# Gate and output projections computed token-major in 512-column groups, in a two-layer decoder kernel on one core

## The chip, the cores and the metric

The kernel runs on one core of one Trainium2 chip. The metric is the device time of one execution in microseconds, as the median of several runs. The engines are called as the profile calls them: PE is TensorE (matmuls; PEld its weight loads), DVE is VectorE, ACT is ScalarE, POOL is GpSimd, SP is SyncE, which issues most DMAs.

## What is computed

Two decoder layers over 256 tokens of width 2048: a gated-linear-attention layer with its ConvFFN, then a cross-attention layer with its ConvFFN. The parts that matter here are the output gate `g` and the two projections back to the residual:

```python
xn = rms_norm(x, norm_w)
proj = xn @ w_in
q, k, v, g = jnp.split(proj, [...], axis=-1)          # g: 2048 columns
...
o = rms_norm(o, o_norm_w) * jax.nn.silu(g.astype(f32)).reshape(B, S, H, dv)
return o.reshape(B, S, GLA_VAL_DIM).astype(x.dtype) @ w_out     # gla_w_out, 2048 x 2048
...
o = o.transpose(1, 0, 3, 2, 4).reshape(B, S, H * Dh)
return o @ w_out                                               # moba_w_out, 2048 x 2048
...
h = h + mixer(...)
h = h + conv_ffn(h, ...)
```

## The kernel before

**Precision.** Every large product is made from split operands: an activation `x` is kept as a high and a low part, side by side, and so is every weight tile. Three of the four products are formed: high weight with both parts of `x`, low weight with the high part.

**Weights.** `WeightStream` loads all weights in one fixed sequence of 1 MB DMAs issued by SP (three raw buffers). A *step* consumes half of such a load, 1024 columns per partition. Before a step's matmuls ACT copies the raw half into `whi` (L144) and DVE subtracts to make `wlo` (L146). Both have four buffers, so the halves for step n can be made when PE has finished with those of step n - 4. `step()` also runs the jobs that are due: `after(k, job)` puts a job k steps ahead. A planner orders the instructions of each engine when the program is built; each engine then runs its list strictly in order.

**Two ways of a product.** `gemm` (L366, L368) is feature-major: the weight is the stationary operand and the result has features on partitions, two blocks of 128 features (a *pair*) by 256 tokens. Its high-weight matmul has 512 moving columns (both parts of 256 tokens), its low-weight one 256. A pair takes four steps. `gemm_tok` (L381, L384) is token-major: the activation is stationary, the weight moves with 512 columns, and the result has tokens on partitions, two tiles of 128 tokens by 512 features. A group of 512 columns takes eight steps. Results lie in `acc` (three buffers in PSUM). Token-major are the v, q, k and kv projections and the two up-projections; feature-major are k and q of the first layer, its gate, and both output projections.

**Turning.** The up-projection turns its token-major result: ACT scales each tile by the tokens' rstd (L720), DVE transposes it in 32 x 32 squares (L722), and `square` (L705) puts the squares in their place with 16 copies on POOL. The rest of the work on it runs 8 and 11 steps later (`UP_LAG`).

**The gate**: for each of eight pairs ACT copies and DVE adds the two halves of `acc` (`both`), DVE multiplies by rstd, ACT applies Silu, DVE multiplies by the head's rstd and by `o` with its norm weight (L627, L629), and `split` makes the operand `go` of the next product (L406, L407).

**The projections** (`project`): for each of eight pairs `residual` adds both halves of `acc` to `h` (L402, L403) and `feed` makes the next norm's operand (`make_xw`, L258, L262) and adds the squares. `Norm.close` makes the rstd from the sum of squares with two matmuls of one column (L307). The operands of a norm are a list in the order of feeding.

**Beside it** `make_ahead` loads parts of `w_dn` every nine steps (`ahead`, two buffers), forms differences on DVE (L329, L330) in four of the steps 5 to 8 after, and writes them back from POOL's queue (`tsum`, L339). `park` writes `h` out on POOL's queue.

Of the kernel before, what the change touches and what calls it, by code (L numbers as in the profile page):

```python
# [18 lines left out]
S = 256  # L19
KT = D // 128  # L20
NP = KT // 2
KD = 1024
VD = 2048
GH = 4
# [7 lines left out]
C_GN, C_KVN, C_MN, C_FN, C_ON, C_KN, C_QN, C_CW = 0, 16, 32, 48, 80, 84, 85, 86  # L32
# [10 lines left out]

UP_LAG = (8, 11)
EARLY = (1, 3)
ASIDE = (5, 7, 9, 11, 13, 15, 16)
# [107 lines left out]


@with_exitstack
def trunk(ctx: ExitStack, tc: tile.TileContext, xT, cst, msk, w1p, w2a, w_k, w_qa, w_v2, w_v, w_g, w_go,
          w_up0, w_dn0, w_kk, w_kv, w_mq, w_mo, w_up1, w_dn1, rel, onehot, out):  # L160
    nc = tc.nc
    V, A, T = nc.vector, nc.scalar, nc.tensor

# [27 lines left out]
    plan = [(w_v2, 1, 16384), (w_v, 2, 8192), (w_k, 4, 4096), (w_qa, 4, 4096), (w_g, 8, 4096), (w_go, 8, 4096),  # L191
            (w_up0, FT // 2, 8192), (w_dn0, 2, None),
            (w_mq, 4, 8192), (w_kk, 4, 8192), (w_kv, 4, 8192), (w_mo, 8, 4096),
            (w_up1, FT // 2, 8192), (w_dn1, 2, None)]
    for w, groups, cols in plan:
        for g in range(groups):
# [8 lines left out]
    h = [hs[p // 2][:, p % 2] for p in range(NP)]  # L205
# [44 lines left out]
    def col(c):  # L250
        return gn[:, c - C_GN:c - C_GN + 1] if C_GN <= c < C_GN + KT else cs[:, c:c + 1]

    def make_xw(p, c, name):
        x = slot([128, 2, 2 * S], F32R, name)
        for i in range(2):
            n = col(c + 2 * p + i)
            if ws.x_low:
                hi = A.activation(x[:, i, :S], h[p][:, i, :], AF.Copy, scale=n)  # L258
                ws.first = ws.first or hi.ins
            else:  # L260
                V.tensor_scalar(x[:, i, :S], h[p][:, i, :], n, None, op0=OP.mult)  # L261
# [59 lines left out]
    def after(steps, job):  # L321
        later.append((cur[0] + steps, job))
# [36 lines left out]
    def gemm(xs, kts):  # L359

        ps = acc_ps.tile([128, 2, 512], F32, name="acc")
        for q0 in range(0, kts, 8):
            two = [step(), step(1)]
            tiles_ = [(q0 + 4 * i + k, b, i, k * 256 + b * 128) for i in range(2) for k in range(4) for b in range(2)]
            for kt, b, i, c in tiles_:
                T.matmul(ps[:, b, :], two[i][0][:, c:c + 128], xs(kt), start=kt == 0, stop=False)  # L366
            for kt, b, i, c in tiles_:
                T.matmul(ps[:, b, :S], two[i][1][:, c:c + 128], xs(kt)[:, :S], start=False, stop=kt == kts - 1)  # L368
        ws.prefetch(cur[0])
        return ps  # L370

    def gemm_tok(xs, groups=1):
        out_ = [acc_ps.tile([128, 2, 512], F32, name="acc") for _ in range(groups)]
        for q0 in range(0, KT, 2):
            for ps in out_:
                hi, lo = step()
                for ks in ((0,), (1,)) if cur[0] < 5 and groups > 1 else ((0, 1),):
                    tiles_ = [(q0 + k, t, k * 512) for k in ks for t in range(2)]
                    for x0 in (0, S):
                        for kt, t, c in tiles_:  # L380
                            T.matmul(ps[:, t, :], xs(kt)[:, x0 + 128 * t:x0 + 128 * t + 128], hi[:, c:c + 512],  # L381
                                     start=kt == 0 and x0 == 0, stop=False)
                    for kt, t, c in tiles_:
                        T.matmul(ps[:, t, :], xs(kt)[:, 128 * t:128 * t + 128], lo[:, c:c + 512],  # L384
                                 start=False, stop=kt == KT - 1)
        ws.prefetch(cur[0])
        return out_ if groups > 1 else out_[0]

    def rows(xs):
        return lambda kt: xs[kt // 2][:, kt % 2, :]  # L390

    def both(ps, name):
        t = temp(name)
        A.copy(t, ps[:, :, S:])
        V.tensor_add(t, t, ps[:, :, :S])
        return t

    def bc(r):
        return r[:, None, :S].to_broadcast([128, 2, S])
# [5 lines left out]
    def split(dst_hi, dst_lo, src):  # L405
        A.copy(dst_hi, src)  # L406
        V.tensor_sub(dst_lo, src, dst_hi.bitcast(F32))  # L407

    class Norm:


        def __init__(self, c, name, rows=True, columns=False):
            self.c, self.name, self.rows, self.columns, self.xs = c, name, rows, columns, []
            self.acc = keep.tile([128, 2, S], F32, name="acc_sq", tag="acc_sq")

        def operand(self, p):
            self.xs.append(make_xw(p, self.c, self.name))

        def feed(self, p):
            self.operand(p)  # L420
# [10 lines left out]
    nrm = Norm(C_GN, "xw", columns=True)  # L431
# [12 lines left out]
    xs = rows(nrm.xs)  # L444
# [81 lines left out]
    for hd in (2, 3):  # L526
        ps = gemm_tok(xs)
# [39 lines left out]
    heads = [{} for _ in range(GH)]  # L567
# [39 lines left out]
    for hd in range(GH):  # L607
        ps = gemm(xs, KT)
# [8 lines left out]
        for lag, job in ((2, gla_scores), (4, gla_values), (6, gla_norm)):  # L617
            after(lag, lambda job=job, hd=hd: job(hd))

    go = []  # L620
    for hd in range(GH):
        for c in range(2):
            ps = gemm(xs, KT)
            g = both(ps, "g")
            V.tensor_mul(g, g, bc(rstd))
            A.activation(g, g, AF.Silu)
            V.tensor_mul(g, g, bc(heads[hd]["r"]))  # L627
            for i in range(2):
                V.scalar_tensor_tensor(g[:, i, :], heads[hd]["o"][:, 2 * c + i, :], col(C_ON + 2 * c + i),  # L629
                                       g[:, i, :], op0=OP.mult, op1=OP.mult)  # L630
            gx = slot([128, 2, 2 * S], F32R, "go")
            split(gx[:, :, :S], gx[:, :, S:], g)
            go.append(gx)

    def project(xs, kts, norms):
# [58 lines left out]
    def combine_parts(k, hid, kept):  # L694
# [5 lines left out]
    def square(y, x):  # L700

        for m in range(4):
            xs_ = x[32 * m:32 * m + 32].rearrange("a t (n c b) -> a n t c b", c=4, b=32)
            for c in range(4):
                nc.gpsimd.tensor_copy(y[32 * c:32 * c + 32, :, :, 32 * m:32 * m + 32], xs_[:, :, :, c])  # L705

    def ffn(layer, nrm, then):
        xs = rows(nrm.xs)
# [5 lines left out]
        def turn_up(g, ps):  # L714
# [10 lines left out]
            for jj in range(2):  # L725
                after(UP_LAG[jj], lambda jj=jj: conv(g, jj, y[:, jj]))

# [350 lines left out]
    xs = rows(n_q.xs)  # L1078
    for g in range(4):
        ps = gemm_tok(xs)  # L1080
# [8 lines left out]
    xs = rows(xkv)  # L1089
    for g in range(4):  # L1090
        ps = gemm_tok(xs)
# [11 lines left out]
    for g in range(4):  # L1103
        ps = gemm_tok(xs)
# [121 lines left out]
```

## Time and profile before

| | us |
|---|---|
| Median of 3 runs | 2176.6 (2175.9 to 2176.62) |
| Profiled execution | 2175.2 |
| Its span, first to last instruction | 2173.4 |
| First output projection, first matmul to the next stage's first | 296.93 to 385.99 |

The granted TensorE clock is 1.00 throughout. The page lists busy times by engine; the chain that ended last follows the work back from the end and says which engine set the time at each moment. A group of instructions is shown as line, engine, operation, output and input, count, then busy time and mean length in ns, then the idle time before it with what ended that idle time. An instruction's length is longer than the distance to the next one where they overlap; the distance between starts is called the pitch here.

### The profile page before, as it was taken

To read this page: it belongs to the slowest core of one execution; us is meant where nothing else is said; L and a number is where in the kernel's file an instruction comes from. 1 tells how busy PE (TensorE), PEld (TensorE's weight loads), DVE (VectorE), ACT (ScalarE), POOL (GpSimd) and SP (SyncE) were. 2 spreads that over 40 slices of the span, in tenths; PEclk is the share of its full clock that TensorE was granted. 3 is DMA by queue.
4 is the path that set the end of the run, shared out by engine and by line. 5 is a ranking of instruction groups with operands and counts; after the bars stand their busy time and mean duration, and the time that the engine had idled before them with its cause. 6 is when DMAs were issued, how large, how long until landed. Compare 5 with 4: busy or idle time off the path is not lost.

```text
span 2173.4 us, 29230 instructions
## 1 busy us (share of the span) xinstructions
PE 2165.5 (100%) x10224; PEld 1815.1 (84%) x10224; DVE 1829.8 (84%) x2531; ACT 1311.9 (60%) x1849; POOL 659.4 (30%) x925
## 2 busy tenths in 40 slices
PE   9999999999999999999999999999999999999999
PEld 7889888888888888887888888888888888888887
DVE  7676877699999897977978787677999999979898
ACT  6655655456565655766756666445565656567575
POOL 0000000264656464300001343003655565542000
PEclk9999999999999999999999999999999999999999
DMA  7575778777778785887967788677787878759896
GB/s 289 209 289 178 263 263 321 287 263 285 273 281 313 275 311 191 329 329 259 366 245 293 275 299 294 228 285 276 284 302 275 310 284 290 293 191 349 325 358 251
DMA packets 113526, 613.01 MB, mean 282 GB/s; under 512 B 29361, under 2 KB 29889, under 8 KB 49634
## 3 DMA queue, kind: packets, MB, share of 16 engines
q1 hardware_dynamic: 94610, 523.75, 66.5%
q0 software_dynamic: 18048, 86.60, 10.5%
q8 instruction: 80, 1.31, 0.2%
q10 hardware_dynamic: 720, 0.79, 0.1%
q14 instruction: 68, 0.56, 0.1%
HBM read 535.31 MB, written 75.78 MB: 281 GB/s over the span
## 4 chain that ended last, share of the span: by engine, by line
PE 98%; DMA 2%; DVE 0%; ACT 0%; issue 0%; ACTq 0%; DVEq 0%; SPq 0%
PE acc L381 40%; PE acc L384 20%; PE acc L803 13%; PE acc L366 11%; PE acc L368 6%; PE p L803 5%; DMA wraw<-w_dn 1%; PE sT L577 0%; DMA sums<-tsum 0%; DMA ahead<-tsum 0%; PE tr L1005 0%; PE s L1023 0%; DVE wlo L146 0%; DMA h<-xT 0%; PE z L483 0%; PE o L463 0%
## 5 line engine op out<-in xcount | busy, mean ns | idle before, releaser
L146 DVE TENSOR_TENSOR wlo<-wraw,whi 128x1024 fp32r<-128x1024 f32 (+1 forms) x788 | 954.3, 1221 | 266.6 <-ACT whi L144 179.8
L144 ACT CAST whi<-wraw 128x1024 fp32r<-128x1024 f32 (+1 forms) x788 | 797.1, 1018 | 611.9 <-PE acc L381 361.8
L381 PE MATMUL acc<-whi,xw 128*128 128x512 f32 x3328 | 825.5, 389 | 0.6 <-DVE xw L261 0.6
L381 PEld LDWEIGHTS acc<-whi,xw 128*128 128x128 f32 x3328 | 623.5, 188 | 130.4 <-issue 1.1
L705 POOL COPY up<-uT 32x256 f32<-32x256 f32 x704 | 520.9, 740 | 310.5 <-DVE uT L722 240.7
L384 PE MATMUL acc<-wlo,xw 128*128 128x512 f32 x1664 | 445.9, 389 | 0.0
L384 PEld LDWEIGHTS acc<-wlo,xw 128*128 128x128 f32 x1664 | 312.1, 188 | 65.0 <-DVE wlo L146 0.3
L339 POOL DMA_DIRECT2D tsum<-ahead x58 | 31.6, 545 | 549.3 <-DVE ahead L330 511.7
L803 PE MATMUL acc<-whi,hid 128*128 128x512 f32 x588 | 168.1, 390 | 1.3 <-ACT whi L144 1.3
L146 DVE TENSOR_TENSOR wlo<-ahead,whi 128x1024 fp32r<-128x1024 f32 x98 | 120.4, 1235 | 19.0 <-ACT whi L144 12.2
L803 PEld LDWEIGHTS acc<-whi,hid 128*128 128x128 f32 x588 | 109.8, 188 | 24.7 <-ACT whi L144 2.3
L381 PE MATMUL acc<-whi,xkv 128*128 128x512 f32 x512 | 129.9, 391 | 0.0
L144 ACT CAST whi<-ahead 128x1024 fp32r<-128x1024 f32 x98 | 101.9, 1054 | 42.9 <-PE p L803 18.5
L366 PE MATMUL acc<-xw,whi 128*128 128x512 f32 x512 | 124.5, 392 | 0.0
L803 PE MATMUL p<-whi,hid 128*128 128x512 f32 x356 | 111.5, 389 | 0.0
L381 PEld LDWEIGHTS acc<-whi,xkv 128*128 128x128 f32 x512 | 95.1, 188 | 18.9
L366 PEld LDWEIGHTS acc<-xw,whi 128*128 128x128 f32 x512 | 93.6, 188 | 17.7
L803 PE MATMUL acc<-whi,comb 128*128 128x512 f32 x348 | 101.3, 390 | 0.7 <-ACT whi L144 0.7
L803 PE MATMUL acc<-wlo,hid 128*128 128x512 f32 x294 | 96.3, 390 | 0.0
L735 ACT ACTIVATE au<-up,cs 128x256 f32<-128x256 f32 x176 | 96.1, 595 | 0.0
L742 DVE SCALAR_TENSOR_TENSOR au<-up,cs,au 128x254 f32<-128x254 f32 x176 | 90.2, 543 | 0.0
L740 DVE SCALAR_TENSOR_TENSOR au<-up,cs,au 128x255 f32<-128x255 f32 x176 | 89.2, 543 | 0.2
(266 smaller groups left out, 2355.3 us busy)
## 6 DMA issues: line engine op xcount, KB each, us to landing
wraw<-w_up SPq DMA_DIRECT2D x176, 1024.0 KB, 5.5
ahead<-w_dn SPq DMA_DIRECT2D x58, 1024.0 KB, 8.9
tsum<-ahead POOLq DMA_DIRECT2D x58, 1024.0 KB, 8.8
ahead<-tsum SPq DMA_DIRECT2D x49, 1024.0 KB, 6.9
wraw<-w_dn SPq DMA_DIRECT2D x58, 768.0 KB, 6.3
wraw<-w_dn SPq DMA_DIRECT2D x30, 1024.0 KB, 6.7
wraw<-w_g SPq DMA_DIRECT2D x16, 1024.0 KB, 4.9
wraw<-w_go SPq DMA_DIRECT2D x16, 1024.0 KB, 6.2
```

Source lines behind the costliest of these rows:

```text
L144: self.high = nc.scalar.copy(hi[:, a:b], src[:, a:b])
L146: self.low = nc.vector.tensor_sub(lo[:, a:b], src[:, a:b], hi[:, a:b].bitcast(F32))
L339: after(8, lambda: nc.gpsimd.dma_start(parked[layer][at], t))
L366: T.matmul(ps[:, b, :], two[i][0][:, c:c + 128], xs(kt), start=kt == 0, stop=False)
L368: T.matmul(ps[:, b, :S], two[i][1][:, c:c + 128], xs(kt)[:, :S], start=False, stop=kt == kts - 1)
L381: T.matmul(ps[:, t, :], xs(kt)[:, x0 + 128 * t:x0 + 128 * t + 128], hi[:, c:c + 512], start=kt == 0 and x0 == 0, stop=False)
L384: T.matmul(ps[:, t, :], xs(kt)[:, 128 * t:128 * t + 128], lo[:, c:c + 512], start=False, stop=kt == KT - 1)
L705: nc.gpsimd.tensor_copy(y[32 * c:32 * c + 32, :, :, 32 * m:32 * m + 32], xs_[:, :, :, c])
L735: A.activation(au[:, i, :], t[:, i, :], AF.Identity, bias=col(cb + n), scale=col(cw + 2 * 2 * FT + n))
L740: V.scalar_tensor_tensor(au[:, i, 1:], t[:, i, :S - 1], col(cw + 2 * FT + n), au[:, i, 1:], op0=OP.mult, op1=OP.add)
L742: V.scalar_tensor_tensor(au[:, i, 2:], t[:, i, :S - 2], col(cw + n), au[:, i, 2:], op0=OP.mult, op1=OP.add)
L803: T.matmul(p[n], x[xi], w[wi][:, 512 * f:512 * f + 512], start=n not in begun, stop=left[n] == 0)
```

## The change

The gate, the first output projection (`gla_w_out`) and the second (`moba_w_out`) are each computed in two manners: columns 0 to 1023 and 1536 to 2047 token-major, as three groups of 512 (groups 0, 1 and 3), and then columns 1024 to 1535 feature-major, as pairs 4 and 5. The weights are laid out for it (`w_gt`, `w_got`, `w_mot` beside shortened `w_g`, `w_go`, `w_mo`). In the gate, ACT applies Silu straight from `acc` with the token's rstd as its scale; in the projections DVE transposes straight from `acc`. POOL then makes 16 copies a group, and the work on pair i of a group runs `LAG + i` steps (8 and 9) after the job that turns it. In the build the two multiplies of a group's `gate_out` stand next to each other in DVE's list. Operands and `go` are dictionaries by pair, since the pairs are no longer made in their order.

```diff
+LAG = 8
...
-    plan = [..., (w_g, 8, 4096), (w_go, 8, 4096),
+    plan = [..., (w_gt, 3, 8192), (w_g, 2, 4096), (w_got, 3, 8192), (w_go, 2, 4096),
...
-            (w_mq, 4, 8192), (w_kk, 4, 8192), (w_kv, 4, 8192), (w_mo, 8, 4096),
+            (w_mq, 4, 8192), (w_kk, 4, 8192), (w_kv, 4, 8192), (w_mot, 3, 8192), (w_mo, 2, 4096),
...
+    def squares(name, xs):
+        x, y = slot([128, 2, 512], F32, name + "T"), slot([128, 4, S], F32, name)
+        for t in range(2):
+            with after_low():
+                V.transpose(x[:, t], xs[t])
+        square(y.rearrange("p n (t s) -> p n t s", t=2), x)
+        return y
...
-    go = []
-    for hd in range(GH):
-        for c in range(2):
-            ps = gemm(xs, KT)
-            g = both(ps, "g")
-            V.tensor_mul(g, g, bc(rstd))
-            A.activation(g, g, AF.Silu)
-            V.tensor_mul(g, g, bc(heads[hd]["r"]))
-            ...
-            go.append(gx)
+    go = {}
+    def gate_out(p, g):
+        hd, c = p // 2, p % 2
+        with after_low():
+            V.tensor_mul(g, g, bc(heads[hd]["r"]))
+        for i in range(2):
+            V.scalar_tensor_tensor(g[:, i, :], heads[hd]["o"][:, 2 * c + i, :], col(C_ON + 2 * c + i),
+                                   g[:, i, :], op0=OP.mult, op1=OP.mult)
+        gx = slot([128, 2, 2 * S], F32R, "go")
+        split(gx[:, :, :S], gx[:, :, S:], g)
+        go[p] = gx
+    def gate_turn(g, ps):
+        us = [temp("g", (128, 512)) for _ in range(2)]
+        for t in range(2):
+            A.activation(us[t], ps[:, t, :], AF.Silu, scale=nrm.col[:, t:t + 1])
+        y = squares("gate", us)
+        for i in range(2):
+            after(LAG + i, lambda i=i: gate_out(2 * g + i, y[:, 2 * i:2 * i + 2]))
+    for g in (0, 1, 3):
+        ps = gemm_tok(xs)
+        after(0, lambda g=g, ps=ps: gate_turn(g, ps))
+    for p in (4, 5):
+        ps = gemm(xs, KT)
+        g = both(ps, "g")
+        V.tensor_mul(g, g, bc(rstd))
+        A.activation(g, g, AF.Silu)
+        gate_out(p, g)
...
     def project(xs, kts, norms):
-        for p in range(NP):
+        def join(p, y):
+            with after_low():
+                V.tensor_add(h[p], h[p], y)
+            for n in norms:
+                n.feed(p)
+        def turn(g, ps):
+            y = squares("out", [ps[:, t, :] for t in range(2)])
+            for i in range(2):
+                after(LAG + i, lambda i=i: join(2 * g + i, y[:, 2 * i:2 * i + 2]))
+        for g in (0, 1, 3):
+            ps = gemm_tok(xs)
+            after(0, lambda g=g, ps=ps: turn(g, ps))
+        for p in (4, 5):
             ps = gemm(xs, kts)
             residual(ps, p)
             for n in norms:
                 n.feed(p)
```

Steps are counted through the whole kernel: the gate has steps 64 to 95 (groups 0, 1, 3 in 64 to 87, pairs 4 and 5 in 88 to 95), the first output projection steps 96 to 127, the first up-projection starts at step 128. In the built order of the changed kernel six of the eight gate_outs (those of groups 1 and 3 and of pairs 4 and 5) stand on DVE between the weights of steps 93 and 104, and PE's list takes step 104 ahead of step 101 and step 105 ahead of the end of step 102.

More of the change, by code (lines that the diff above doesn't have):

```diff
@@ L158, in trunk @@
 @with_exitstack
-def trunk(ctx: ExitStack, tc: tile.TileContext, xT, cst, msk, w1p, w2a, w_k, w_qa, w_v2, w_v, w_g, w_go,
-          w_up0, w_dn0, w_kk, w_kv, w_mq, w_mo, w_up1, w_dn1, rel, onehot, out):
+def trunk(ctx: ExitStack, tc: tile.TileContext, xT, cst, msk, w1p, w2a, w_k, w_qa, w_v2, w_v, w_gt, w_g, w_got, w_go,
+          w_up0, w_dn0, w_kk, w_kv, w_mq, w_mot, w_mo, w_up1, w_dn1, rel, onehot, out):
     nc = tc.nc
@@ L190, in trunk @@
         parked.append({at: t[n] for n, at in enumerate(todo)})
-    plan = [(w_v2, 1, 16384), (w_v, 2, 8192), (w_k, 4, 4096), (w_qa, 4, 4096), (w_g, 8, 4096), (w_go, 8, 4096),
+    plan = [(w_v2, 1, 16384), (w_v, 2, 8192), (w_k, 4, 4096), (w_qa, 4, 4096), (w_gt, 3, 8192), (w_g, 2, 4096), (w_got, 3, 8192), (w_go, 2, 4096),
             (w_up0, FT // 2, 8192), (w_dn0, 2, None),
-            (w_mq, 4, 8192), (w_kk, 4, 8192), (w_kv, 4, 8192), (w_mo, 8, 4096),
+            (w_mq, 4, 8192), (w_kk, 4, 8192), (w_kv, 4, 8192), (w_mot, 3, 8192), (w_mo, 2, 4096),
             (w_up1, FT // 2, 8192), (w_dn1, 2, None)]
@@ L387, in gemm_tok, with square @@
         return out_ if groups > 1 else out_[0]
+    def square(y, x):
+        for m in range(4):
+            xs_ = x[32 * m:32 * m + 32].rearrange("a t (n c b) -> a n t c b", c=4, b=32)
+            for c in range(4):
+                nc.gpsimd.tensor_copy(y[32 * c:32 * c + 32, :, :, 32 * m:32 * m + 32], xs_[:, :, :, c])
+    def squares(name, xs):
[5 more added lines that the diff above has]
+        return y
     def rows(xs):
@@ L412, in __init__ @@
         def __init__(self, c, name, rows=True, columns=False):
-            self.c, self.name, self.rows, self.columns, self.xs = c, name, rows, columns, []
+            self.c, self.name, self.rows, self.columns, self.xs = c, name, rows, columns, {}
             self.acc = keep.tile([128, 2, S], F32, name="acc_sq", tag="acc_sq")
         def operand(self, p):
-            self.xs.append(make_xw(p, self.c, self.name))
+            self.xs[p] = make_xw(p, self.c, self.name)
         def feed(self, p):
@@ L618, in trunk, with project @@
             after(lag, lambda job=job, hd=hd: job(hd))
-    go = []
-    for hd in range(GH):
-        for c in range(2):
-            ps = gemm(xs, KT)
-            g = both(ps, "g")
-            V.tensor_mul(g, g, bc(rstd))
-            A.activation(g, g, AF.Silu)
-            V.tensor_mul(g, g, bc(heads[hd]["r"]))
-            for i in range(2):
[L629 to L632, printed above, removed]
-            go.append(gx)
-    def project(xs, kts, norms):
-        for p in range(NP):
+    go = {}
+    def gate_out(p, g):
+        hd, c = p // 2, p % 2
+        with after_low():
+            V.tensor_mul(g, g, bc(heads[hd]["r"]))
+        for i in range(2):
[20 more added lines that the diff above has]
+        gate_out(p, g)
+    def project(xs, kts, norms):
+        def join(p, y):
[5 more added lines that the diff above has]
+            y = squares("out", [ps[:, t, :] for t in range(2)])
+            for i in range(2):
+                after(LAG + i, lambda i=i: join(2 * g + i, y[:, 2 * i:2 * i + 2]))
[3 more added lines that the diff above has]
+        for p in (4, 5):
             ps = gemm(xs, kts)
@@ L698, in combine_parts @@
         combine(k, hid[k], [(t[:, i, :128], t[:, i, 128:]) for i in range(2)], kept)
[L700 to L705, printed above, removed]
     def ffn(layer, nrm, then):
@@ L1184, in slab, with outer @@
         return np.ascontiguousarray(t.reshape(NP, 2, 128, S).transpose(0, 2, 1, 3)).reshape(NP, 128, 2 * S)
+    def outer(w):
+        return np.concatenate([w[:, :1024], w[:, 1536:]], axis=1)
     cst = np.concatenate(
@@ L1203 @@
         "w_v": _groups(win[:, 2 * KD + VD // 2:2 * KD + VD], 512),
-        "w_g": _groups(win[:, 2 * KD + VD:], 256),
-        "w_go": _groups(a["gla_w_out"][0], 256),
+        "w_gt": _groups(outer(win[:, 2 * KD + VD:]), 512),
+        "w_g": _groups(win[:, 2 * KD + VD:][:, 1024:1536], 256),
+        "w_got": _groups(outer(a["gla_w_out"][0]), 512),
+        "w_go": _groups(a["gla_w_out"][0][:, 1024:1536], 256),
         "w_up0": _groups(_interleaved(a["ffn_w_up"][0]), 512),
@@ L1210 @@
         "w_mq": _groups(a["moba_w_q"][0], 512),
-        "w_mo": _groups(a["moba_w_out"][0], 256),
+        "w_mot": _groups(outer(a["moba_w_out"][0]), 512),
+        "w_mo": _groups(a["moba_w_out"][0][:, 1024:1536], 256),
         "w_up1": _groups(_interleaved(a["ffn_w_up"][1]), 512),
```

## The prediction

> **What bounds the kernel now.** I read the page's busy times, the chain that ended last, and then who kept PE (TensorE) waiting.
>
> ```profile
> PE 2165.5 (100%) x10224; PEld 1815.1 (84%) x10224; DVE 1829.8 (84%) x2531; ACT 1311.9 (60%) x1849; POOL 659.4 (30%) x925
> PE 98%; DMA 2%; DVE 0%; ACT 0%; issue 0%; ACTq 0%; DVEq 0%; SPq 0%
> ```
> ```profile
> PE acc L803 <- ACT whi L144: 1.9, 3, 1.3
> PE junk L218 <- POOL idle L215: 1.3, 1, 1.3
> PE acc L381 <- DVE xw L261: 0.6, 1, 0.6
> ```
>
> PE is busy for 2165.5 of 2173.4 us and is 98% of the chain; all its waits for other engines add up to 3.8 us, none of them in the gate or the projections. So only two things can move the time: the pitch at which matmuls follow each other in the changed groups, and new holes in PE's stream. The pitch is read from the starts in the chain, first feature-major (output projection, L366 and L368), then token-major (up-projection, L381 and L384).
>
> ```profile
> 296.93 3.65 PE acc L366 x16
> ...
> 313.62 3.65 PE acc L366 x16
> 317.27 1.91 PE acc L368 x16
> ...
> 363.72 3.65 PE acc L366 x16
> ```
> ```profile
> 385.99 1.84 PE acc L381 x8
> ...
> 402.84 1.81 PE acc L381 x8
> 404.65 0.91 PE acc L384 x4
> ...
> 457.24 1.81 PE acc L381 x8
> ```
>
> Feature-major, two steps take (363.72 - 313.62)/9 = 5.567 us, so a pair of output blocks (four steps) 11.13 us; the whole stage agrees: (385.99 - 296.93)/8 = 11.13. Token-major a step takes (457.24 - 402.84)/20 = 2.720 us. Per instruction that is 3.65/16 = 228 ns for 512 columns and 1.91/16 = 119 ns for 256: more than half, so a short matmul carries the same overhead over fewer columns.
>
> **The change part by part.** *PE.* A 512-column group replaces two pairs: 22.27 us become 8 x 2.720 = 21.76 us, because 64 matmuls of 256 columns become 32 of 512. The gain is 0.507 us a group, 4.56 us for nine. No other matmul is added or removed. Bounds: 0 (the groups would run at the old pitch) to 4.56; I take 4.56, since the 44 groups of the two up-projections have these very shapes, and PE has no waits there.
>
> The Trainium skill speaks against it (TensorE: Matmul & The Clock Gate, section Back-to-back issue gap): it gives a gap of N/2.4 + 2.5 ns, by which 32 instructions fewer save an estimated 0.08 us a group, 0.7 us in all. The rows disagree: 228 ns for 512 columns is 12 ns more than that gap, and 119 is 10 ns more.
>
> *VectorE (DVE), ScalarE (ACT) and GpSimd (POOL).*
>
> ```profile
> L722 DVE STREAM_TRANSPOSE uT<-up 128x512 f32<-128x512 f32 x88 | 58.3, 693 | 0.0
> L403 DVE TENSOR_TENSOR h<-h,acc 128x512 f32<-128x512 f32 x16 | 10.9, 684 | 0.1
> L625 DVE TENSOR_TENSOR g<-g,rstd_h 128x512 f32<-128x512 f32 x8 | 5.4, 690 | 0.1
> L395 DVE TENSOR_TENSOR g<-g,acc 128x512 f32<-128x512 f32 x8 | 5.4, 685 | 0.1
> L394 ACT COPY g<-acc 128x512 f32<-128x512 f32 x8 | 4.6, 584 | 2.2 <-PE acc L368 2.2
> ```
> ```profile
> L705 POOL COPY up<-uT 32x256 f32<-32x256 f32 x704 | 520.9, 740 | 310.5 <-DVE uT L722 240.7 <-PE acc L384 22.3 <-issue 20.0
> ```
>
> A gate group loses two adds and two multiplies on DVE (2 x 685 + 2 x 690 = 2.75 us) and two copies on ACT (1.17 us), and gains two transposes (1.39 us); ACT now applies rstd in the Silu. A projection group trades four adds from PSUM (2.74 us) for two transposes and two adds (2.75 us). A transpose out of PSUM is not in this trace; the add out of PSUM (684) costs what the one out of SBUF does (690), so I take 693. POOL gains 16 copies a group, 144 x 0.74 = 107 us, off PE's chain. Weights come in as many DMAs of the same size. The loss of the deeper prefetch on these weights costs nothing: the up-projection runs without it and PE never waits there.
>
> *What the copies do to DVE.* The two rows are the same instruction, in the projection (no copies) and in the up-projection (copies half the time).
>
> ```profile
> L146 DVE TENSOR_TENSOR wlo<-wraw,whi 128x1024 fp32r<-128x1024 f32 x31 | 37.2, 1223 | 19.6 <-issue 12.7 <-PE acc L368 6.8
> ```
> ```profile
> L146 DVE TENSOR_TENSOR wlo<-wraw,whi 128x1024 fp32r<-128x1024 f32 x169 | 223.2, 1322 | 42.2 <-ACT whi L144 41.9
> ```
> ```profile
> 520.60 1.42 DVE L146 TENSOR_TENSOR wlo<-wraw,whi 128x1024 fp32r<-128x1024 f32 x1
> 533.67 1.22 DVE L146 TENSOR_TENSOR wlo<-wraw,whi 128x1024 fp32r<-128x1024 f32 x1 [0.52 <-ACT whi L144]
> ```
> ```profile
> 520.51 12.90 POOL L705 COPY up<-uT 32x256 f32<-32x256 f32 x16 [3.23 <-DVE uT L722]
> 1952.56 14.41 POOL L705 COPY up<-uT 32x256 f32<-32x256 f32 x16 [8.95 <-DVE uT L722]
> ```
>
> While 16 copies run (12.9 us from 520.51), the low half of a weight takes 1.42 instead of 1.22 us. So in the gate and projections DVE is some 16% slower for about 13 of each 21.8 us. On average there is room: the windows below (stage, its length, busy time and instructions of PE, its weight loads, DVE, ACT and POOL) have DVE at 63.9 of 86 us in the output projection, and at 428.8 of 478 in the up-projection, which carries it. What counts is where DVE is bunched.
>
> ```profile
> 300.00:386.00 86.00, 86.00 (x500) 76.21 (x499) 63.89 (x82) 42.87 (x54) 5.43 (x10) 1.00 0.83 304
> 390.00:868.00 478.00, 478.00 (x2112) 395.97 (x2111) 428.77 (x586) 285.01 (x403) 259.40 (x363) 1.00 0.76 277
> ```
>
> *The wait that the change adds.* A join or gate_out waits for its copies eight steps (21.8 us) after the group. Its chain is about 1.3 us of transposes (two), 12.9 of copies, 1.2 of a weight in between and the ACT eviction: some 17 us, so 5 us are spare. Behind a waiting join DVE queues the low halves of the weights, and PE waits for those.
>
> *Where DVE is bunched: the start of the first output projection.* In the built order the gate_outs of groups 1 and 3 and of the two feature-major pairs, six of eight, fall into 12 steps, and PE's order there is rearranged: step 104 (the next group's first) is pulled ahead of step 101. Time zero is PE's first projection matmul (step 96). Four buffers let DVE start the weight of step n when PE has finished n-4. DVE pitches, from starts without a dependence:
>
> ```profile
> 297.21 0.69 DVE L407 TENSOR_TENSOR go<-g,go 128x512 fp32r<-128x512 f32 x1
> 297.81 1.22 DVE L146 TENSOR_TENSOR wlo<-wraw,whi 128x1024 fp32r<-128x1024 f32 x1
> 298.95 0.68 DVE L395 TENSOR_TENSOR g<-g,acc 128x512 f32<-128x512 f32 x1
> 304.51 0.88 DVE L629 SCALAR_TENSOR_TENSOR g<-o,cs,g 128x256 f32<-128x256 f32 x2
> ```
>
> 0.60 us for 512 elements, 1.14 for a weight, 0.40 for 256. With step 98's weight done at 1.25 (it starts when PE frees step 94, at -0.95, behind an overrun of 0.8 and at copy speed), DVE has before it six weights (6.8), ten operations of 512 (6.0) and eight of 256 (3.3): 16.1, and 0.4 for the copies of group 3 that still run. Step 104's low half is ready at 17.8. PE wants it after five steps (13.6), 0.2 for the high half, eight matmuls of step 104 (1.8) and four of step 101 (0.9): 16.5. I charge 1.3 us of stall. Below: 0, if DVE gains 1.3 us on these pitches. Above, with the full durations (1.22, 0.69, 0.48) 18.1 instead of 16.1: 3.3. I take the pitches because most neighbours are independent.
>
> *Elsewhere.* Where up-projections begin, pair 5 is needed in step 5 (13.6 us in) and the joins of 6 and 7 in steps 6 and 7; from 4.9 us, after pair 4 and the join of 6 and 7, DVE has three weights, five operations of 512 and six of 256 before it (10.0 at full durations), so the low half of step 6 is ready at 14.9 against 18.1 wanted. Cost nothing, covered by 3.2 us; without that cover what exceeds it, twice. The two-column sum goes from step 5 to the end of step 7 of the up-projection, with its sum ready at 18.4 (two more weights, one of 512, one of 256) of 21.5. Attention's projection starts with nothing but two splits on DVE. POOL's writes of parked sums queue behind copies, and SP's next load of w_dn behind those:
>
> ```profile
> ahead<-w_dn SPq DMA_DIRECT2D x58, 1024.0 KB, 8.9
> tsum<-ahead POOLq DMA_DIRECT2D x58, 1024.0 KB, 8.8
> ```
>
> A buffer is held for 8 steps (22 us, the 8.9 of the load among them) and 8.8 of write; two buffers at one load per 9 steps give 49. A delay by a group's copies (13) fits.
>
> *Sum.* Profiled execution 2175.2 us (span 2173.4 and 1.8 around): 2175.2 - 4.56 + 1.3 = 2171.9. It lies 1.4 below the median of the runs, 2176.6; on the median's scale **2173.3**.
>
> **The rivals.** *Full cover* (0.25): the stall is nothing, 2172.0. For it: PE idles nowhere at the same place today. Against: six gate_outs in 12 steps.
>
> *Old pitch* (0.08): the groups gain nothing and the stall stays, 2177.9. The page on TensorE named above goes this way. Against: the rows of L381 and L384.
>
> *Copies held up by DVE* (0.15), slower.
>
> ```profile
> L705 POOL COPY up<-uT x704: 392/496/1478, 411.6 to 1965.7; 32x256 f32<-32x256 f32 x176
> ```
>
> A single copy takes 392 to 1478 ns, so it waits for something of the length of a DVE operation. If in the denser gate stage all 16 took 1.478, 23.6 us, a chain would be 23.6 + 4 = 27.6, 5.8 beyond its eight steps, and DVE, then PE, would stand for it. In the three gate groups alone that is 17.4: 2173.3 + 17.4 = 2190.7. It decides from 18 us for 16 copies (1.12 each); the longest here is 14.41. The Trainium skill (SBUF — State Buffer, section Who interferes with whom) calls the port that DVE and GpSimd share an exclusive lock, whose loser blocks; the spread of the copies agrees, the 1.42 for 1.22 only in direction.
>
> **How the numbers follow.** The forecast has 0.52. What a measurement tells from no change is 0.2%, 4.35 us: faster means below 2172.25, which only full cover and the lucky edge of the forecast reach, 0.28; slower means above 2180.95, 0.15, from the held copies; the rest, 0.57, is within. Range: from full cover less 0.6 for the spread of the runs, 2171.4, past the stall's upper bound (2175.3) and the old pitch to 2179.5; above that lies most of the slower rival.
>
> **What would show it.** Right: token-major steps of 2.72 us in gate and both projections; 288 fewer PE matmuls; one PE hole of 0 to 3 us near the first projection's fifth step, put down to the low half of a weight; POOL groups of 12 to 14 us. Wrong: a step of 2.78; PE waiting at every group, behind a join on POOL; or PE holes at the starts of the up-projections.

## The result and the profile after

| | before | after |
|---|---|---|
| Median of 20 runs each, us | 2175.96 (2173.74 to 2178.89) | 2172.78 (2170.98 to 2174.45) |
| Ratio, 95% interval | | 0.9985 (0.9979 to 0.9991) |
| Profiled execution, us (its span) | 2175.2 (2173.4) | 2173.0 (2171.2) |

The median is 3.2 us lower, and the interval of the ratio excludes 1. The forecast was 2173.3.

The first view is the page of the changed kernel: busy time, instructions, and the shares of the chain that ended last.

```profile
PE 2162.0 (100%) x9936; PEld 1800.0 (83%) x9936; DVE 1839.8 (85%) x2525; ACT 1301.2 (60%) x1840; POOL 771.9 (36%) x1069
...
PE 97%; DMA 1%; DVE 1%; issue 0%; ACT 0%; ACTq 0%; DVEq 0%
```

PE has 288 matmuls fewer (10224 - 9936) and 3.5 us less work, POOL 112 us more. DVE, which was 0% of the chain, is now 1%: somewhere the end is set by DVE. The chain between 230 and 330 us shows where (start, length, what).

```profile
243.54 1.81 PE acc L382 x8
...
270.74 1.81 PE acc L382 x8
273.46 3.63 PE acc L367 x16
...
295.70 1.84 PE acc L382 x8
...
306.61 1.81 PE acc L382 x8
308.84 1.58 DVE gate L645 x4
310.42 1.14 DVE wlo L147
312.16 1.15 DVE wlo L147
313.35 1.20 PE acc L385 x4
```

The gate's token-major steps are (270.74 - 243.54)/10 = 2.720 us apart, as in the up-projection, and the first projection begins in the same rhythm. Thirteen microseconds into it the chain leaves PE for 4.5 us of DVE work. PE's timeline at that place, with idle time and what ended it in brackets, prices the hole:

```profile
295.54 2.00 PE L382 MATMUL acc<-whi,go 128*128 128x512 f32 x8
...
308.26 1.07 PE L385 MATMUL acc<-wlo,go 128*128 128x512 f32 x4
309.61 3.01 PE L382 MATMUL acc<-whi,go 128*128 128x512 f32 x12 [0.28 <-ACT whi L145]
313.35 1.20 PE L385 MATMUL acc<-wlo,go 128*128 128x512 f32 x4 [0.73 <-DVE wlo L147]
314.38 1.07 PE L382 MATMUL acc<-whi,go 128*128 128x512 f32 x4
```

Four matmuls take 0.91 us at the pitch of 2.720/12 = 0.2267. So the twelve of 309.61 were due at 308.26 + 0.91 = 309.17 and came 0.44 late; the four low-weight ones were due at 309.61 + 2.72 = 312.33 and came 1.02 late; and those four then took 1.03 to the next start instead of 0.91. Together 1.58 us. The brackets show only 1.01: idle time counts from the end of a matmul that overlaps the next one, so a hole is read from starts.

DVE's timeline shows what it was doing (the last row is the weight that PE waited for):

```profile
287.98 0.88 DVE L424 TENSOR_TENSOR go<-gate,go 128x512 fp32r<-128x512 f32 x1
288.78 0.67 DVE L412 TENSOR_TENSOR g<-g,acc 128x512 f32<-128x512 f32 x1
289.38 0.72 DVE L424 TENSOR_TENSOR go<-gate,go 128x512 fp32r<-128x512 f32 x1
290.02 1.41 DVE L147 TENSOR_TENSOR wlo<-wraw,whi 128x1024 fp32r<-128x1024 f32 x1
...
295.09 2.75 DVE L147 TENSOR_TENSOR wlo<-wraw,whi 128x1024 fp32r<-128x1024 f32 x2
...
305.03 1.28 DVE L643 TENSOR_TENSOR gate<-gate,rstd_o 128x512 f32<-128x512 f32 x2
306.24 1.21 DVE L147 TENSOR_TENSOR wlo<-wraw,whi 128x1024 fp32r<-128x1024 f32 x1
307.37 0.67 DVE L330 TENSOR_TENSOR ahead<-ahead 128x512 f32<-128x512 f32 x1
307.97 0.86 DVE L645 SCALAR_TENSOR_TENSOR g<-o,cs,g 128x256 f32<-128x256 f32 x2
308.77 1.66 DVE L645 SCALAR_TENSOR_TENSOR gate<-o,cs,gate 128x256 f32<-128x256 f32 x4
310.35 1.21 DVE L147 TENSOR_TENSOR wlo<-wraw,whi 128x1024 fp32r<-128x1024 f32 x1
...
312.09 1.21 DVE L147 TENSOR_TENSOR wlo<-wraw,whi 128x1024 fp32r<-128x1024 f32 x1
```

No row has an idle time in brackets: DVE is not waiting, it is full. Between the end of the pitch of the weight at 306.24 and the next one at 310.35 lie 3.0 us of a parked difference (`make_ahead`) and six half-size products of gate_outs. The first of the two weights at 295.09 is step 98's, the one at 312.09 is step 104's. By pitches the work after the former, to the end of the latter, is 16.0 us (six weights, ten operations of 512 and eight of 256); it took 16.9, and the difference lies before 302, beside the copies. POOL's timeline has the copies:

```profile
243.21 11.52 POOL L395 COPY gate<-gateT 32x256 f32<-32x256 f32 x16 [2.21 <-DVE gateT L402]
...
286.30 15.19 POOL L395 COPY gate<-gateT 32x256 f32<-32x256 f32 x16 [8.27 <-DVE gateT L402]
325.10 13.33 POOL L395 COPY out<-outT 32x256 f32<-32x256 f32 x16 [5.70 <-DVE outT L402]
```

The three product stages, measured from the first matmul of each to the first of the next stage (the gate's with the first layer's k and q, which the change leaves alone):

| Stage, us | before | after | difference |
|---|---|---|---|
| k, q and gate | 197.44 | 196.01 | -1.43 |
| First output projection | 89.05 | 89.14 | +0.09 |
| Second output projection | 91.34 | 89.92 | -1.42 |

The up-projections take 479.25 to 479.26 in both.

### The profile page after: what moved, and what is told of

The parts are those of the page before. It is cut to its first block, busy times and chain, and to the rows that moved or that the text cites. A ratio compares the mean times of both kernels' runs of the same rounds, so it can differ in the third digit from the quotient of the medians.

```text
span 2171.2 us, 28783 instructions
## 1 busy us (share of the span) xinstructions
PE 2162.0 (100%) x9936; PEld 1800.0 (83%) x9936; DVE 1839.8 (85%) x2525; ACT 1301.2 (60%) x1840; POOL 771.9 (36%) x1069
## 4 chain that ended last, share of the span: by engine, by line
PE 97%; DMA 1%; DVE 1%; issue 0%; ACT 0%; ACTq 0%; DVEq 0%
PE acc L382 46%; PE acc L385 23%; PE acc L844 13%; PE p L844 5%; PE acc L367 5%; PE acc L369 2%; DMA ahead<-tsum 1%; DMA wraw<-w_dn 1%; PE sT L594 0%; DVE wlo L147 0%; PE tr L1046 0%; PE s L1064 0%; DMA h<-xT 0%; ACT whi L145 0%; PE z L500 0%
## 5 line engine op out<-in xcount | busy, mean ns | idle before, releaser
L382 PE MATMUL acc<-whi,xw 128*128 128x512 f32 x3520 | 873.0, 390 | 0.6 <-DVE xw L262 0.6
L382 PEld LDWEIGHTS acc<-whi,xw 128*128 128x128 f32 x3520 | 659.3, 188 | 138.0 <-issue 1.3
L385 PE MATMUL acc<-wlo,xw 128*128 128x512 f32 x1760 | 472.5, 389 | 0.0
L385 PEld LDWEIGHTS acc<-wlo,xw 128*128 128x128 f32 x1760 | 330.1, 188 | 68.6 <-DVE wlo L147 0.3
L331 DVE TENSOR_TENSOR ahead<-ahead 128x512 f32<-128x512 f32 x116 | 87.0, 750 | 0.3
L330 DVE TENSOR_TENSOR ahead<-ahead 128x512 f32<-128x512 f32 x116 | 86.9, 750 | 0.3
```

What stands on the lines that cost most here:

```text
L330: jobs = [lambda: V.tensor_sub(b22, b22, b12), lambda: V.tensor_sub(b12, b12, b11), lambda: V.tensor_add(b11, b22, b11), lambda: V.tensor_ ...
L331: lambda: V.tensor_add(b11, b22, b11), lambda: V.tensor_sub(b21, b21, b11)]
```

## The experiments

The theory: the pitch gives about 1.5 us in each of the three stages, and the first projection gives its share back because DVE, with six gate_outs close together, is late with one weight. The rivals: the hole belongs to the token-major projection itself; it is the copies that make it, by slowing DVE; DVE's amount of work there makes it, and not its order; the late operands of the last group make it. Two more runs price the rival "copies held up" and the cause of the pitch. All ratios are against the kernel before, with 95% intervals.

| Run | k, q, gate | first projection | second | time / before | ratio |
|---|---|---|---|---|---|
| before | 197.44 | 89.05 | 91.34 | | |
| changed kernel | 196.01 | 89.14 | 89.92 | 2172.78 / 2175.96 | 0.9985 (0.9979 to 0.9991) |
| proj_only | 197.44 | 87.54 | 89.92 | 2174.15 / 2175.58 | 0.9992 (0.9983 to 1.0001) |
| gate_only | 196.01 | 94.44 | 91.35 | 2179.51 / 2175.58 | 1.0017 (1.0009 to 1.0026) |
| no_copies | 196.02 | 88.12 | 89.93 | 2171.29 / 2175.58 | 0.9978 (0.9968 to 0.9987) |
| gate_lag10 | 196.01 | 87.54 | 89.93 | 2170.66 / 2175.58 | 0.9975 (0.9966 to 0.9984) |
| ahead28 | 196.01 | 91.30 | 89.92 | 2175.16 / 2175.15 | 1.0000 (0.9990 to 1.0010) |
| copies_twice | 196.01 | 104.11 | 89.92 | 2215.31 / 2175.15 | 1.0185 (1.0170 to 1.0200) |
| all_tok | 195.53 | 94.92 | 89.44 | 2185.05 / 2175.15 | 1.0047 (1.0032 to 1.0062) |
| low128 | 194.14 | 87.51 | 89.70 | 2171.18 / 2175.15 | one run |
| after_2 | 196.01 | 89.14 | 89.93 | 2172.44 / 2175.78 | 0.9984 (0.9975 to 0.9993) |
| lag10_2 | 196.01 | 87.55 | 89.92 | 2170.20 / 2175.78 | 0.9974 (0.9963 to 0.9984) |

### The projections alone

```diff
-    for g in (0, 1, 3):
-        ps = gemm_tok(xs)
-        after(0, lambda g=g, ps=ps: gate_turn(g, ps))
-    for p in (4, 5):
...
+    for hd in range(GH):
+        for c in range(2):
+            ps = gemm(xs, KT)
...
+            go.append(gx)
```

> Only the two output projections are token-major; the gate is that of before. Theory (pitch gain 0.507 us a group, and one hole at the start of the first projection that comes from the bunched gate_outs on DVE): six groups give 3.04 us, and no hole, since the gate's work on DVE is spread as before: ratio to before 0.9986, about 2172.9 us. Rival A (the hole belongs to the token-major first group of the projection, whatever the gate does): hole of 1.0 to 1.6 us stays, 1.5 to 2 us gained, ratio 0.9992. Rival B (no gain of pitch): ratio 1.000.

The first projection takes 87.54 us, 1.51 less than before, and PE waits nowhere in it. The token-major projection has no hole of its own; behind the old gate DVE has enough lead: in the first 17.8 us of the projection it is busy for 14.45 us with 18 instructions, where in the changed kernel it is busy throughout with 26. PE's order differs too: behind the old gate no step is pulled ahead there. The measured ratio is the one that rival A named, but its interval holds the theory's as well and just reaches 1, so it is the stage that decides here.

### The gate alone

```diff
-        for g in (0, 1, 3):
-            ps = gemm_tok(xs)
-            after(0, lambda g=g, ps=ps: turn(g, ps))
-        for p in (4, 5):
+        for p in range(NP):
             ps = gemm(xs, kts)
```

> Only the gate is token-major; both projections are those of before. Theory: three groups give 1.52 us; but a feature-major first pair needs the operands of pairs 6 and 7 in its third and fourth step (from 5.6 us on) where DVE has their low parts only some 19 us in, so PE stands for several us at that place: hole of 3 to 8 us, time 2177.5 to 2182.5, ratio 1.0007 to 1.003. Rival A (the bunch on DVE does not matter): 1.5 us faster, ratio 0.9993.

The gate keeps its -1.43, but the first projection is 5.39 longer than before. PE's timeline of this run:

```profile
306.25 2.00 PE L367 MATMUL acc<-go,whi 128*128 128x512 f32 x8
311.74 6.43 PE L367 MATMUL acc<-go,whi 128*128 128x512 f32 x20 [3.49 <-DVE go L424]
```

Here PE waits for the operand `go` itself, not for a weight, and the twenty matmuls behind the hole take 6.3 us to the next start where 4.6 would do (see the last section). A feature-major pair runs over all of `go` within four steps (11.1 us), a token-major group within eight (21.8); so the new gate, whose last operands come late, needs the new projection behind it. DVE works without a pause from before 290 until that operand is there (311.7), so the bunch of gate_outs does harm here too, by another wait.

### Without the copies

The 16 copies of each gate and projection group are left out, so those features stand in the wrong places.

```diff
-        x, y = slot([128, 2, 512], F32, name + "T"), slot([128, 4, S], F32, name)
+        x = slot([128, 2, 512], F32, name + "T")
...
-        square(y.rearrange("p n (t s) -> p n t s", t=2), x)
-        return y
+        return x.rearrange("p t (n s) -> p (t n) s", s=S)
```

> The kernel after, without the 16 copies on POOL in the gate and projections: the transposed tile is used as it lies, so the features of these groups are in the wrong places; every other instruction stays. Theory: DVE runs at full speed in the gate (about ten operations 0.2 us shorter), the hole at the start of the first projection shrinks from 1.3 to 0 to 0.4 us, and the time is before less 4.2 to 4.6 us: ratio 0.9979 to 0.9981, about 2171.5. Rival A (DVE's own amount of work makes the hole, the copies have no part): hole stays at 1 us or more, ratio 0.9985 as after. Rival B (copies cost in all nine groups): more than 4.6 us gained.

The hole shrinks from 1.60 to 88.12 - 87.54 = 0.58 us, a little more than the 0 to 0.4 expected, and only the wait for ACT's high half is left:

```profile
309.59 3.02 PE L382 MATMUL acc<-whi,go 128*128 128x512 f32 x12 [0.28 <-ACT whi L145]
```

This doesn't show that the copies cost 1.0 by slowing DVE. Without them the planner also put the two multiplies of group 3's gate_outs at 295.96 instead of 305.03, and DVE's work between the weights of steps 98 and 104 is 14.0 us by pitches instead of 16.0. A slower DVE and more work on it aren't told apart by this run.

### The gate's second half two steps later

```diff
         for i in range(2):
-            after(LAG + i, lambda i=i: gate_out(2 * g + i, y[:, 2 * i:2 * i + 2]))
+            after(10 + i, lambda i=i: gate_out(2 * g + i, y[:, 2 * i:2 * i + 2]))
```

> The kernel after with the gate's work on a turned pair 10 and 11 steps after instead of 8 and 9. Theory: the two gate_outs of group 3 stand apart and behind those of pairs 4 and 5, DVE is bunched less before step 104, and the hole is 0 to 0.7 us: 2171.5 to 2172.3, ratio 0.9979 to 0.9983. Rival A (later operands of pairs 6 and 7 make PE wait for them instead): hole of 2 to 4 us, 2173.5 to 2175.5.

The hole is gone: 87.54 us, no wait of PE in the projection. PE's timeline and then DVE's:

```profile
308.99 1.98 PE L382 MATMUL acc<-whi,go 128*128 128x512 f32 x8
...
311.71 3.79 PE L382 MATMUL acc<-whi,go 128*128 128x512 f32 x16
```
```profile
297.54 0.69 DVE L643 TENSOR_TENSOR gate<-gate,rstd_o 128x512 f32<-128x512 f32 x1
...
299.54 1.22 DVE L147 TENSOR_TENSOR wlo<-wraw,whi 128x1024 fp32r<-128x1024 f32 x1
300.67 0.68 DVE L643 TENSOR_TENSOR gate<-gate,rstd_o 128x512 f32<-128x512 f32 x1
...
308.07 0.68 DVE L330 TENSOR_TENSOR ahead<-ahead 128x512 f32<-128x512 f32 x1
308.68 0.68 DVE L424 TENSOR_TENSOR go<-g,go 128x512 fp32r<-128x512 f32 x1
309.28 1.28 DVE L424 TENSOR_TENSOR go<-gate,go 128x512 fp32r<-128x512 f32 x2
310.48 1.21 DVE L147 TENSOR_TENSOR wlo<-wraw,whi 128x1024 fp32r<-128x1024 f32 x1
```

The theory had group 3's gate_outs come later, behind those of pairs 4 and 5. They came 5.0 to 7.5 us earlier, because the planner also turned group 3 earlier: its copies run from 276.01 to 289.20, not from 286.30 to 301.49. So the hole went, but not in the way that was expected.

It is not DVE's order alone that took it away. Between the weights of steps 98 and 104 DVE has nearly the same work as in the changed kernel, 15.8 us by pitches instead of 16.0, and it took just these 15.8 where it took 16.9 beside the copies. With step 98's weight done 0.45 us sooner, step 104's (the row at 310.48) was ready 16.3 us after the projection's first matmul instead of 17.8. PE's order changed as well: it takes step 101 at 308.99 and only then step 104, whose high half ACT makes from 308.62 to 309.67. That ends the wait for the high half and puts off the need for the low one. The run doesn't tell these apart; but 16.3 would have been in time for the changed kernel's order too, where the low half was wanted at 16.8.

The time, 2170.66, is below the expected range; the interval of the ratio covers that range. The median is the lowest of all runs so far; the last experiment compares it with the changed kernel on one chip.

### One prefetch job elsewhere

```diff
-    make_ahead(0, w_dn0, 24, 9)
+    make_ahead(0, w_dn0, 28, 9)
```

> The kernel after, with LAG 8 as it is, and only the loads of w_dn ahead started four steps later (28 instead of 24), so that their differences on DVE fall elsewhere. Theory (the hole is DVE's bunch before step 104, whatever makes it): the first output projection takes 87.5 to 87.9 us instead of 89.14, the whole 1 to 1.6 us less than after: ratio to before 0.9975 to 0.9982. Rival A (the lag itself, by which pairs 6 and 7 come late, makes the hole): projection still 88.8 or more.

A miss. Moving the parked differences out of the bunch was to shrink the hole, and the loss grew to 91.30 - 87.54 = 3.8 us. PE's timeline:

```profile
303.20 1.21 PE L382 MATMUL acc<-whi,go 128*128 128x512 f32 x4 [1.48 <-DVE go L424]
...
312.41 2.12 PE L382 MATMUL acc<-whi,go 128*128 128x512 f32 x8 [0.62 <-ACT go L423]
```

The planner made another order: group 3 is transposed only at 301.28 (it was at 284.85), its copies start at 302.74, and now the operands are late and no weight is. The edit did not clear the place either. It moved one set of four differences out and the one before it in: DVE makes four in the first 14 us of the projection (295.62, 299.54, 305.21, 308.42), where the changed kernel makes three up to step 104's weight (297.77, 307.37, 311.49). So the run says nothing on whether the amount of DVE's work makes the hole. What it shows is that late operands can cost more than a late weight. The 91.3 lies where rival A put it, but the operands are late by the later turning, at the same lag.

### The copies twice

```diff
-        square(y.rearrange("p n (t s) -> p n t s", t=2), x)
+        for _ in range(2):
+            square(y.rearrange("p n (t s) -> p n t s", t=2), x)
```

> The kernel after with every copy of the gate and projections made twice, 32 a group: some 26 us a group, past the 18 us from which the prediction's slower case decides. Theory: a chain of 30 us against 21.8 holds DVE up to 8 us at each join; DVE stands up to three steps (8 us) ahead of PE, so single holds are half absorbed: 10 to 50 us slower than after, 2183 to 2223. Rival A (the planner moves the joins, since it knows of the copies): under 5 us slower. Rival B (nothing absorbed): nine times 8, 72 us slower.

Now 32 copies take 24 to 27 us, beyond the 21.8 that a chain has. POOL's timeline and PE's:

```profile
278.88 27.30 POOL L395 COPY gate<-gateT 32x256 f32<-32x256 f32 x32 [10.31 <-PE acc L369]
310.47 24.82 POOL L395 COPY gate<-gateT 32x256 f32<-32x256 f32 x32 [3.80 <-DVE gateT L402]
```
```profile
309.06 3.62 PE L382 MATMUL acc<-whi,go 128*128 128x512 f32 x8 [8.08 <-ACT go L424]
...
411.98 3.78 PE L382 MATMUL acc<-whi,xw 128*128 128x512 f32 x8 [6.89 <-ACT xw L259]
```

The first projection grows by 15.0 us over the changed kernel, the up-projections by 14.6 and 10.3, the kernel by some 43. So a chain longer than its eight steps does hold up PE, as the slower rival had it, and this sets in somewhere between 15.2 and 24 us of copies; the changed kernel stays below it. That DVE alone stretches 16 copies so far was seen in no run. PE does not stand at every group but where a stage takes the last operands of the one before.

### All four groups token-major

```diff
-LAG = 8
+LAG = 5
...
-    for g in (0, 1, 3):
+    for g in range(4):
...
-    for p in (4, 5):
-        ps = gemm(xs, KT)
...
-            after(2, n.close)
+            after(LAG + 2, n.close)
```

The projections' loops change in the same way.

> Gate and both projections wholly token-major, four groups each, no feature-major pairs; work on a turned pair 5 and 6 steps after. Theory: three more groups give 1.5 us of pitch, but the last group's chain (17 us and then the operand's five operations) ends some 22 us into the next stage, where pairs 6 and 7 are wanted 16.3 and 19 us in; the planner can pull one or two steps of the next group ahead: holes of 2 to 8 us at three places, 2176 to 2192. Rival A (the planner hides it all): 2169.9, ratio 0.997.

```profile
310.46 3.78 PE L382 MATMUL acc<-whi,go 128*128 128x512 f32 x8 [4.80 <-ACT go L423]
```

The gate gains another 0.48 us and the second projection too, as the pitch says (0.51 a group). But the last group's copies have nothing to hide behind, even with the chain cut from eight steps to five: the first projection is 5.8 us longer than in the changed kernel and the first up-projection 3.7 (482.93). Another 4.9 us are lost between the first down-projection and the second output projection, where PE's waits add up to 3.1 us (0.5 in the changed kernel); the rest stays open. The time is in the expected range; holes were expected at three places and came at two, none at the second up-projection (479.23). The two feature-major pairs pay for themselves.

### A shorter low-weight matmul in the kernel before

The low-weight product of the feature-major matmuls is left out for tokens 128 to 255.

```diff
-                T.matmul(ps[:, b, :S], two[i][1][:, c:c + 128], xs(kt)[:, :S], start=False, stop=kt == kts - 1)
+                T.matmul(ps[:, b, :128], two[i][1][:, c:c + 128], xs(kt)[:, :128], start=False, stop=kt == kts - 1)
```

> The kernel before, with the low-weight matmuls of all feature-major products cut from 256 to 128 columns, so that tokens 128 to 255 lack that product. Theory A (a matmul's pitch is its columns and a fixed 12 ns): 119 ns become 66, the output projection loses 256 x 53 ns = 13.6 us, the whole 54 us. Theory B (a short matmul is bound by the load of its stationary operand, about 110 ns as the 128-column ones of the value products show): 119 become 108 to 112, the output projection loses 2 to 3 us, the whole 7 to 12.

The chain of this run, in the first projection:

```profile
315.30 1.74 PE acc L368 x16
317.04 3.74 PE acc L366 x16
```

Half the columns take 1.74/16 = 109 ns instead of 119, and the matmuls of 512 beside them 234 instead of 228. Theory A's 66 ns are excluded: at 128 columns the pitch is not the columns and a fixed 12 ns. A floor near 109 ns, as theory B has it, fits; its times do not, since the 512s grew: the first projection lost 1.5 us where 2 to 3 were expected, and the whole 4.0 where 7 to 12 were. Between 256 and 512 columns this run decides nothing: 119 and 228 also agree with about 109 ns for each 256 columns and a fixed 10. Why a matmul of 256 takes more than half of one of 512 stays open.

### The changed kernel and the later gate side by side

Both once more, on one chip, unchanged.

> The kernel after once more, beside the next on one chip. Theory: ratio 0.9985 to before, with the hole of 1.6 us in the first output projection (89.1 us).

> The kernel with the gate's lag of 10 once more. Theory: no hole (projection 87.5 us), 1.6 us below the kernel after of the same call, ratio to before 0.9975 to 0.9980. Rival (the difference of 2.1 us between the medians of the earlier calls was the chip's): equal to the kernel after within 0.5 us.

The hole comes back at the same place and with the same size (89.14 against 87.55). The medians are 2.2 us apart, 2172.44 and 2170.20, where 1.6 was expected; the intervals overlap, so it is the two profiles of each, 1.59 to 1.60 us apart in this one stage, that show the difference.

## Why the prediction was right

*What bounds it.* PE does, before and after. Both quantities that could move the time, the pitch and a new hole, did.

*The pitch, 4.56 us.* The steps came out at 2.720. The stages gave 1.43, 1.51 (from the runs without the hole) and 1.42, together 4.36; each is up to 0.1 short of three times 0.507. The two that are short have attention's small matmuls in between and the first projection has none; whether that is why was not tried. Of the 0.507 a group, 0.39 are from the merging, 32 times 2 x 119.4 - 226.7 ns; the rest is that the 64 matmuls that had 512 columns all along follow at 226.7 instead of 228 ns. The bound 0, and with it the rival "old pitch", is excluded. The rule cited for it from the Trainium skill (TensorE: Matmul & The Clock Gate, section Back-to-back issue gap) would have given 0.7 us for all nine groups; it is given there for an isolated matmul, and the runs, with 4.36, do not agree.

*The stall, 1.3 us.* Place and cause were right, and the size nearly. Counted from the projection's first matmul (295.54), the low half was ready at 313.30, that is 17.8 as forecast, and wanted at 312.33, 16.8 instead of 16.5. The high half was 0.44 late where 0.2 was put in, and the restart of 0.12 was not in the sum: 1.6 instead of 1.3. That the 17.8 came out to the tenth is luck, since two errors cancel in it: DVE was done with step 98's weight at about 0.9 instead of 1.25, and the copies of group 3, 15.2 us long and running to 301.49, cost 0.8 us instead of 0.4. As 0.9 and the 16.0 of work make 16.9, hardly more than the 16.8 at which PE wanted the weight, the 0.8 from the copies is most of the 1.0 that it came late: the bunch used up the room, and the copies went beyond it. The prediction treated the copies' share as a small correction.

*The other work of DVE, ACT and POOL at nothing.* Right. The transpose out of PSUM, which no row showed, takes 692 ns by the groups of the changed kernel:

```profile
L402 DVE STREAM_TRANSPOSE outT<-acc 128x512 f32<-128x512 f32 x12 | 7.8, 692 | 2.1 <-PE acc L385 2.1
L395 POOL COPY gate<-gateT 32x256 f32<-32x256 f32 x48 | 37.3, 777 | 22.7 <-DVE gateT L402 20.8
L395 POOL COPY out<-outT 32x256 f32<-32x256 f32 x96 | 73.6, 767 | 32.3 <-PE acc L369 10.8 <-PE acc L382 10.2 <-DVE outT L402 6.2
```

The copies take 777 and 767 ns where 740 was used, 111 us in all (107), and of the groups, for which 12 to 14 us were expected, one took 15.2 and one 11.5. The doubled copies show what cover this rests on.

*Elsewhere.* The starts of both up-projections, the moved two-column sum and the queues past POOL cost nothing: those stages are unchanged to 0.01 us.

*The sum.* On the profiled execution 2171.9 was forecast and 2173.0 measured. Of the 1.1 the pitch is 0.2, the stall 0.3; the rest, 0.6, lies in stages that the change does not touch (the last one, from the second down-projection's first matmul to the end, took 225.76 instead of 225.31, and between 225.0 and 226.3 in other runs). The median fell by 3.2 where the stages give 1.43 - 0.09 + 1.42 = 2.8; the interval of the ratio reaches from 2.0 to 4.6 us, so nothing is to be explained there. The forecast meant 3.3 us less than before; that the medians differ by so nearly the same is in part luck, since the stages make it 2.8.

*The rivals.* Full cover was not the case, but is 1.6 us away, by one constant. Copies held up so long that PE stands at every group did not occur at 16 copies a group.

Not borne out is a half-sentence on the cause of the pitch, that a short matmul carries the same overhead over fewer columns: it fits 256 and 512 columns, and fails at 128. The sum, made from measured pitches, didn't rest on it.

## What to carry to other kernels

Price a new tiling by the starts of instructions of the same shape elsewhere in the trace, and a hole by starts too, not by the idle times in brackets. Where an engine at 85% feeds a saturated one with a lead of four buffers, list its instructions in the built order between two of the weights it makes: a bunch of a few microseconds costs what its average load hides. Price it at the pace that the engine has beside the others' work at that place, here POOL's copies. Moving one due time or one prefetch can remove the hole or trade it for a larger one. When a scheduler builds the order, try neighbouring constants and read the order that comes out, since the one meant to help may do the opposite.

## What the hardware showed

A long hole costs more than its length. In the run with four token-major groups, the windows around the hole (window, its length, busy time and instructions of PE, its weight loads, DVE, ACT and POOL, then the granted clock):

```profile
300.00:305.00 5.00, 5.00 (x24) 4.14 (x23) 3.05 (x3) 1.67 (x3) 3.05 (x6) 1.00 0.84 310
305.00:310.40 5.40, 0.67 (x3) 0.20 (x2) 4.52 (x8) 1.46 (x2) 0.00 (x0) 0.92 0.57 196
310.40:315.70 5.30, 5.24 (x12) 4.18 (x13) 2.52 (x5) 1.67 (x3) 2.97 (x7) 0.50 0.16 66
```

After a wait of 4.80 us the clock is 0.50 for 5.3 us, and twelve matmuls take 5.3 us instead of 2.7, the next eight 2.2 instead of 1.8: the hole of 4.9 us by starts costs 7.9. With the gate alone, a wait of 3.49 was followed by clocks of 0.55 and 0.66. The holes of 1.6 us in the changed kernel and of up to 1.6 us at a time in ahead28 (3.8 in all) left the clock at 1.00. The Trainium skill (TensorE: Matmul & The Clock Gate, section What's actually happening) puts the change at an idle window of about 3.4 us; these four runs agree.

A matmul of 128 moving columns follows the one before after 109 ns, of 256 after 119, of 512 after 227 to 228 (234 beside those of 128). The Trainium skill (TensorE: Matmul & The Clock Gate, section LDWEIGHTS (loading the stationary operand)) gives the stationary load as its columns divided by 1.2, 107 ns for 128. The floor of 109 agrees; that the load is what sets it was not tried by itself.

While POOL copies, most of DVE's operations with two inputs in SBUF take about 0.2 us longer (1.41 instead of 1.21 for 1024 elements, 0.88 instead of 0.67 for 512), and the add with one input in PSUM takes 0.67 in the middle of the same copies (the row at 288.78). The operation right behind that add is hardly slowed (0.72 at 289.38). The Trainium skill (SBUF — State Buffer, section Who interferes with whom) says that one SBUF input doesn't contend with GpSimd and two do: the rows agree, but for the one at 289.38. It also calls the shared port an exclusive lock; the 0.2 us that a DVE operation loses is less than the shortest of the copies (0.39). Whether it waits for the rest of a copy or runs more slowly is not told apart here.
